# State-space layer of a four-layer trunk: input products of 64 states at a time, input copies divided by partitions, lagged copies placed behind the gelus, second half of the gate's product on other banks

## The chip, the cores and the metric

The kernel runs on one core of one Trainium2 chip. The metric is the device time of one execution in microseconds (us), here the median of three runs: 1214.68 us, from 1214.11 to 1215.03. One more execution was recorded by the hardware profiler; all rows quoted below come from that one.

Engines are named as the profile names them: PE is TensorE (PEld its weight loads), DVE is VectorE, ACT is ScalarE, POOL is GpSimd, SP is SyncE, which here only starts transfers.

## The reference

256 tokens of width 1024 pass through four layers. Each has a token mixer (stick-breaking attention, a chunked gating unit, a state-space layer, attention again) and a gated MLP. The change touches the third mixer alone:

```python
def s5_layer(xn, w_in, lam_re, lam_im, log_dt, b_re, b_im, c_re, c_im, d_skip, w_glu):
    u = (xn @ w_in).astype(jnp.float32)
    ug = u.reshape(B, L, SSM_GROUPS, SSM_GROUP)          # 64 groups of 16 channels, 64 states each
    ...
    bu_re = jnp.einsum('gph,blgh->blgp', bbar_re, ug)
    bu_im = jnp.einsum('gph,blgh->blgp', bbar_im, ug)
    ...
    _, _, xr, xi = lax.associative_scan(_complex_affine_combine, (a_re, a_im, bu_re, bu_im), axis=1)
    y = (jnp.einsum('ghp,blgp->blgh', c_re, xr) - jnp.einsum('ghp,blgp->blgh', c_im, xi))
    y = y.reshape(B, L, D_MODEL) + d_skip * u
    hg = jax.nn.gelu(y).astype(xn.dtype) @ w_glu
    a, g = jnp.split(hg, 2, axis=-1)
    return a * jax.nn.sigmoid(g)
```

## The kernel before

The whole trunk is one stream of instructions, written out by hand: every engine works through its own instructions in the order in which the Python code issues them, and an instruction waits only for the counters that its tiles need. So the order of calls in the code is the order on each engine. A tile from a pool with one buffer can be written again only when all readers of its last content are done.

**Large products.** A weight of 1 MB (128 x 2048 fp32) is loaded into one of three `raw` buffers by SP (line 40), rounded by ACT into `wh` (line 71, two halves), and DVE forms the remainder `wl` (line 72, two halves). `Weights.prep_to(i)` issues these for all weights up to the i-th; the load of a weight that needs a `raw` buffer starts when line 72 is through with the weight that held it. A product is three matmuls (`wh` with the high part, `wl` with the high part, `wh` with the low part: lines 132 to 134).

**The state-space layer** is class `S5`. Four tokens are taken together, so that the scan runs over 64 steps, and its body works in four parts of 16 groups, i = 0 to 3. Two of them share one buffer U[h].

- `ucopy(h)` copies the projected input from PSUM into U[h], 16 copies of 32 partitions x 256. For h = 0 ACT and DVE share them, for h = 1 ACT makes them all.
- `gmm(i)` multiplies the input by the input tables: for each of 8 columns a, real and imaginary part r, and block q of 32 states one matmul of 32 x 64.
- `scan(i)`, on DVE with a part on POOL, takes the two banks of `gmm(i)` and gives the state X[i], lines 1147 to 1171.
- `kmm(n)`, `kd(n)` and `kevac(n)` make the table of the lagged products inside a block of four tokens: matmuls (line 1180), a diagonal added by DVE (line 1185), and 16 copies by ACT (line 1192) into `kk[n]`; the tile of `kk[1]` is named `wl` in the rows.
- `ymm(i, parts)` forms the output of part i: its part `K_` uses `kk[i // 2]` and U, its part `X_` uses X[i] (all of it line 1205).
- `yevac(i)`: ACT applies the gelu (line 1213, tile `y`) and rounds it (line 1216, `gh`); DVE forms the remainder (line 1217, `gl`). The tile `y` comes from the pool of the layer, which has one buffer.
- `glu(c, n, acc, bs)` is the last product, 24 matmuls for both token blocks b, into the banks `acc[b]`. The four parts of the first output half use banks (0, 1) and (3, 4); `gate(b, ...)` then takes them out with a sigmoid on ACT (line 1284) and two steps on DVE (lines 1285 and 1286). The second half uses `self.acc`; its part 0 stands at the end of the body, its parts 1 to 3 in `tail`, first for b = 0, then for b = 1, and in between ACT and DVE do the norm of the next layer, whose transposes (line 179) go to two banks given in `run`.

In the body before, `kevac(0)` and `kevac(1)` stand inside `scan(0)` and `scan(1)`; `yevac(0)` and the splitting of the next weight stand ahead of `scan(2)`; the first half's two gates stand behind the splitting of all four weights of the second half; and b = 1 of the second half's part 0 writes banks 0 and 1, which the gate of b = 0 reads.

Of the kernel before, what the change touches and what calls it, by code (L numbers as in the profile page):

```python
# [21 lines left out]
class Weights:  # L22


    def __init__(self, nc, raw_p, hl_p, srcs, ahead_dma, ahead_prep):
        self.nc, self.raw_p, self.hl_p = nc, raw_p, hl_p
        self.srcs = srcs
        self.ad, self.ap = ahead_dma, ahead_prep
        self.raw, self.hl = {}, {}
        self.nd = self.npz = 0  # L30
        self.use = 0
# [66 lines left out]
class K:  # L98
# [131 lines left out]
    def run(self):  # L230
        nc, w = self.nc, self.w
        self.x = self.big.tile([128, 2, D], F32, name="x")
        self.ident = self.const.tile([128, 128], F32, name="ident")
        self.mhalf = self.const.tile([128, 1], F32, name="mhalf")
        nc.gpsimd.memset(self.mhalf[:, :], -0.5)
        zero = self.act_p.tile([128, 512], BF16, tag="gh", name="zero")
        nc.vector.memset(zero[:, :], 0.0)
        for c in (slice(0, 512), slice(512, D)):
            nc.sync.dma_start(self.x[:, 0, c], self.ins["x"][0][:, c])
        g = self.load_g(self.plan[0].g)  # L240
        nc.sync.dma_start(self.ident[:, :], self.ins["ident"])
        nc.sync.dma_start(self.x[:, 1], self.ins["x"][1])
        w.dma_to(3)

        def warm(n):

            for i in range(n):
                nc.tensor.matmul(self.bank(4), zero[:, 0:128], zero[:, :], start=True, stop=True)

        warm(12)  # L250
        self.s5 = next((p for p in self.plan if isinstance(p, S5)), None)
        prev = None
        nop = lambda: None
        for pi, ph in enumerate(self.plan + [None]):
            if prev:
                g = self.load_g(ph.g if ph else 8)
                prev.tail(0, nop)
                if ph:
                    w.prep_to(w.use + 2)
                xn0 = self.norm(0, g, prev.resid)  # L260
                if ph:
                    w.prep_to(w.use + 3)
                    prev.tail(1, lambda: (self.new_xt(), self.to_xt(0, xn0, (5, 6))))
                else:
                    nc.sync.dma_start(self.out[0], xn0[:, :])
                    prev.tail(1, nop)
                xn1 = self.norm(1, g, prev.resid)
                prev.close()
                if not ph:
                    for q, c in ((nc.sync, slice(0, 512)), (nc.scalar, slice(512, D))):  # L270
                        q.dma_start(self.out[1][:, c], xn1[:, c])
                    break
            else:
                xn = [self.norm(b, g) for b in range(2)]
                self.new_xt()
                w.half()
                self.xt_tr(0, xn[0], 0, 5)
                self.xt_evac(0, 0, 5)
                self.xt_tr(0, xn[0], 1, 6)
                warm(8)  # L280
                w.half()
                self.xt_tr(1, xn[1], 0, 0)
                self.xt_evac(1, 0, 0)
                self.xt_tr(1, xn[1], 1, 1)
                ph.open()
                h = ph.first()
                next(h)
                next(h)
                self.xt_evac(0, 1, 6)
                self.xt_evac(1, 1, 1)  # L290
                w.prep_to(2)
                ph.background()
                for _ in h:
                    w.step()
                Attn.consts(self)
                w.prep_to(w.use + 4)
                ph.body()
                prev = ph
                continue
            if ph is self.s5:  # L300
                self.s5.finish_tables()
            ph.open()
            if ph is self.s5:
                w.prep_to(w.use + 6)
            ph.head(0, lambda: self.to_xt(1, xn1, (0, 1)))
            w.prep_to(w.use + 2)
            ph.head(1, nop)
            w.prep_to(w.use + (3 if isinstance(ph, FFN) else 4))
            ph.body()
            prev = ph  # L310


class Phase:
    def __init__(self, k, i, g):
        self.k, self.i, self.g = k, i, g
        self.nc, self.ctx = k.nc, ExitStack()
# [415 lines left out]


class S5(Phase):
    def __init__(self, k, i, g):
        super().__init__(k, i, g)
        self.done = 0
        d = k.dram
        self.d_gt = d.tile([128, 2, 2, 2048], F32, name="d_gt")
        self.d_p = d.tile([128, 2, 2, 2048], F32, name="d_p")  # L740
        self.d_b = d.tile([128, 2048], F32, name="d_b")
        self.d_w = d.tile([8, 2, 32, 64], F32, name="d_w")
        self.d_t = [d.tile([128, 2048], F32, name=f"t{r}") for r in range(2)]
        self.d_s = d.tile([128, 1024], F32, name="d_s")
        self.par = k.const.tile([128, 19, 32], F32, name="spar")
# [355 lines left out]
    def body(self):  # L1101
        k, nc, w = self.k, self.nc, self.k.w
        ut = k.pst[:, 4:8, :].rearrange("p b (a t) -> p (b a) t", a=2)
        n = w.take()
# [17 lines left out]
        GT = [[v4(t[r]) for t in (gt0, gt1)] for r in range(2)]  # L1122
# [3 lines left out]
        X, U = {}, []  # L1126
        gb = lambda i, r: k.bank(((0, 1), (2, 5), (0, 1), (2, 7))[i][r])

        def gmm(i):

            for a in range(8):
                h, c = (8 * i + a) // 16, (8 * i + a) % 16
                for r in range(2):
                    for q in range(4):
                        nc.tensor.matmul(gb(i, r)[32 * q:32 * q + 32, 64 * a:64 * a + 64],
                                         GT[r][h][:, c, 32 * q:32 * q + 32], U[h][:, c, :],
                                         start=True, stop=True, skip_group_check=True)

        def scan(i, mid=lambda: None):
# [43 lines left out]
        def kd(n):  # L1183
            d = k.bank(3 + n).rearrange("p (a c) -> p a c", a=4)[:, :, 0:32]
            nc.vector.tensor_tensor(out=d, in0=d, in1=self.di[:, 4 * n:4 * n + 4], op=add)

        def kevac(n):
            kt = k.bank(3 + n).rearrange("p (a c) -> p a c", a=4)
            kk = self.kk[n][:, :, :, :].rearrange("p (a q) j c -> p q a (j c)", q=4)
            for jp in range(4):  # L1190
                for q in range(4):
                    nc.scalar.activation(kk[32 * jp:32 * jp + 32, q, :, 32 * jp:128],  # L1192
                                         kt[32 * q:32 * q + 32, :, 0:128 - 32 * jp], AF.Copy)
# [16 lines left out]
        def yevac(i):  # L1210
            p = k.bank(6 - i % 2)
            y = self.tmp.tile([128, 2, 256], F32, tag="y", name="y")
            nc.scalar.activation(y[:, :, :].rearrange("p m (c j) -> p m j c", j=4),
                                 p.rearrange("p (m j c) -> p m j c", m=2, j=4), AF.Gelu_apprx_tanh)
            g = self.gt[i] = k.new_gt()
            nc.scalar.activation(g[0][:, :, :], y[:, :, :], AF.Copy)
            nc.vector.tensor_tensor(out=g[1][:, :, :], in0=y[:, :, :], in1=g[0][:, :, :], op=sub)

        def ucopy(h, halves):
            d = U[h].rearrange("p (m r) c -> p m r c", m=4)  # L1220
            for pr in range(4):
                for j in range(4):
                    src = ut[32 * pr:32 * pr + 32, 4 * h:4 * h + 4].rearrange("p m (c j) -> p m c j", j=4)[:, :, :, j]
                    dst = d[32 * j:32 * j + 32, :, pr, :]
                    if halves and pr % 2:
                        nc.vector.tensor_copy(dst, src)
                    else:
                        nc.scalar.activation(dst, src, AF.Copy)
# [10 lines left out]
        scan(0, lambda: (kd(0), kevac(0)))  # L1239
        gmm(2)  # L1240
        kmm(1)
        scan(1, lambda: (kd(1), kevac(1)))
        ymm(0, K_ + X_)
        yevac(0)
        gmm(3)
        ymm(1, K_ + X_)
        w.prep_to(w.use + 2)
        scan(2)
        yevac(1)
        ymm(2, K_)  # L1250
        acc = [(k.bank(0), k.bank(1)), (k.bank(3), k.bank(4))]
        self.glu(0, w.take(), acc, (0, 1))
# [5 lines left out]
        self.glu(1, w.take(), acc, (0, 1))  # L1258
        ymm(3, X_)
        yevac(3)  # L1260
        for i in (2, 3):
            w.prep_to(w.use + 2)
            self.glu(i, w.take(), acc, (0, 1))
            w.step()
        for b in range(2):
            self.gate(b, acc[b], k.x[:, b, 0:512])
        self.acc = [(k.bank(2), k.bank(7)), (k.bank(0), k.bank(1))]
        self.glu(0, w.take(), self.acc, (0, 1))
        w.step()

# [105 lines left out]
```

## Time and profile before

| what | value |
|---|---|
| median of three runs | 1214.68 us |
| the profiled execution, its own time | 1214.6 us |
| its span, first to last instruction | 1212.8 us |
| PE busy | 1175.3 us, 97% of the span |
| DVE busy | 891.9 us, 74% |
| ACT busy | 705.7 us, 58% |
| POOL busy | 162.2 us, 13% |
| mean granted clock of PE | 0.994 of full speed |

A row of the timeline or of the chain of waits begins with the time from the start of the span and the duration, both in us. In a timeline row a bracket at the end gives the time for which the engine stood idle before it, and what ended that. "issue" is time in which PE waited for nothing that the profile shows.

### The profile page before, as it was taken

To read this page: it belongs to the slowest core of one execution; us is meant where nothing else is said; L and a number is where in the kernel's file an instruction comes from. 1 tells how busy PE (TensorE), PEld (TensorE's weight loads), DVE (VectorE), ACT (ScalarE), POOL (GpSimd) and SP (SyncE) were. 2 spreads that over 40 slices of the span, in tenths; PEclk is the share of its full clock that TensorE was granted. 3 is DMA by queue.
4 is the path that set the end of the run, shared out by engine and by line. 5 is a ranking of instruction groups with operands and counts; after the bars stand their busy time and mean duration, and the time that the engine had idled before them with its cause. 6 is when DMAs were issued, how large, how long until landed. Compare 5 with 4: busy or idle time off the path is not lost.

```text
span 1212.8 us, 22510 instructions
## 1 busy us (share of the span) xinstructions
PE 1175.3 (97%) x9328; PEld 1078.3 (89%) x9328; DVE 891.9 (74%) x1276; ACT 705.7 (58%) x1068; POOL 162.2 (13%) x308
## 2 busy tenths in 40 slices
PE   8999999999999999999967899999999999999997
PEld 5898999999898999999956699999988988999996
DVE  5665699789767599899478759876766656886673
ACT  5665576557554564668373657565555655665551
POOL 3885000000285001000111000000000000000000
PEclk8999999999999999999999999999999999999999
DMA  8623467787665356677761725645535332564530
GB/s 296 222 106 122 150 218 267 250 286 259 230 213 206 140 210 227 233 260 272 309 250 38 295 107 180 242 170 194 196 119 224 119 123 108 208 244 174 208 122 35
DMA packets 49559, 237.49 MB, mean 196 GB/s; under 512 B 14896, under 2 KB 15792, under 8 KB 24240
## 3 DMA queue, kind: packets, MB, share of 16 engines
q1 hardware_dynamic: 46208, 223.73, 51.4%
q0 software_dynamic: 3104, 12.06, 2.5%
q8 instruction: 73, 1.20, 0.4%
q14 instruction: 30, 0.25, 0.1%
q10 hardware_dynamic: 144, 0.26, 0.1%
HBM read 222.79 MB, written 13.24 MB: 195 GB/s over the span
## 4 chain that ended last, share of the span: by engine, by line
PE 91%; DVE 4%; ACT 2%; issue 1%; DMA 1%; POOL 0%; DVEq 0%; SPq 0%; POOLq 0%; ACTq 0%
PE pst L124 15%; PE pst L126 15%; PE pst L125 15%; PE pst L132 13%; PE pst L133 13%; PE pst L134 13%; PE pst L534 1%; PE pst L179 1%; DVE wl L72 1%; PE pst L510 1%; PE pst L551 1%; DVE wl L68 1%; ACT wl L1192 1%; DMA raw<-in_glu_dram 1%; DMA gb<-in_g_dram 1%
## 5 line engine op out<-in xcount | busy, mean ns | idle before, releaser
L72 DVE TENSOR_TENSOR wl<-raw,wh 128x1024 fp32r<-128x1024 f32 x344 | 414.8, 1231 | 58.7 <-ACT wh L71 58.5
L124 PE MATMUL pst<-xth,wh 128*128 128x256 f32 x1552 | 441.7, 285 | 0.0
L126 PE MATMUL pst<-xth,wl 128*128 128x256 f32 x1552 | 439.9, 283 | 0.0
L125 PE MATMUL pst<-xtl,wh 128*128 128x256 f32 x1552 | 439.9, 283 | 0.0
L71 ACT ACTIVATE wh<-raw 128x1024 fp32r<-128x1024 f32 x344 | 350.4, 1048 | 9.9 <-DMA raw<-in_glu_dram 4.4
L124 PEld LDWEIGHTS pst<-xth,wh 128*128 128x128 f32 x1552 | 298.1, 192 | 2.3
L125 PEld LDWEIGHTS pst<-xtl,wh 128*128 128x128 f32 x1552 | 298.2, 192 | 1.2
L126 PEld LDWEIGHTS pst<-xth,wl 128*128 128x128 f32 x1552 | 298.1, 192 | 0.0
L408 DVE SCALAR_TENSOR_TENSOR y<-pst,cw,y 128x255 f32<-128x255 f32 x352 | 160.8, 479 | 72.8 <-ACT y L404 66.5
L132 PE MATMUL pst<-wh,gh 128*128 128x512 f32 x512 | 202.5, 396 | 6.1 <-DVE gate L1285 4.5
L133 PE MATMUL pst<-wl,gh 128*128 128x512 f32 x512 | 200.8, 392 | 0.1
L134 PE MATMUL pst<-wh,gl 128*128 128x512 f32 x512 | 200.2, 391 | 0.0
L404 ACT ACTIVATE y<-pst,cw 128x256 f32<-128x256 f32 x176 | 88.0, 556 | 69.4 <-PE pst L126 64.8
L132 PEld LDWEIGHTS pst<-wh,gh 128*128 128x128 f32 x512 | 96.6, 189 | 26.3 <-DVE gate L1285 4.9
L134 PEld LDWEIGHTS pst<-wh,gl 128*128 128x128 f32 x512 | 96.6, 189 | 20.9 <-DVE gl L688 0.4
L133 PEld LDWEIGHTS pst<-wl,gh 128*128 128x128 f32 x512 | 96.8, 189 | 18.6 <-DVE wl L72 0.4
L132 PE MATMUL pst<-wh,xth 128*128 128x256 f32 (+1 forms) x336 | 106.1, 316 | 0.0
L134 PE MATMUL pst<-wh,xtl 128*128 128x256 f32 (+1 forms) x336 | 105.4, 314 | 0.0
L133 PE MATMUL pst<-wl,xth 128*128 128x256 f32 (+1 forms) x336 | 105.4, 314 | 0.0
L163 POOL TENSOR_TENSOR r<-m,mhalf 128x1 f32<-128x1 f32 x20 | 11.0, 552 | 687.6 <-DVE m L161 679.1
L414 ACT ACTIVATE y<-y 128x256 f32<-128x256 f32 x88 | 36.4, 419 | 76.2 <-DVE y L408 76.2
L198 ACT ACTIVATE gh<-y 128x256 fp32r<-128x256 f32 x88 | 36.1, 418 | 75.2 <-DVE y L415 75.2
(179 smaller groups left out, 1203.3 us busy)
## 6 DMA issues: line engine op xcount, KB each, us to landing
raw<-in_up_dram SPq DMA_DIRECT2D x88, 1024.0 KB, 4.9
raw<-in_down_dram SPq DMA_DIRECT2D x44, 1024.0 KB, 4.9
raw<-in_wqk_dram SPq DMA_DIRECT2D x16, 1024.0 KB, 5.4
raw<-in_wo_dram SPq DMA_DIRECT2D x8, 1024.0 KB, 4.8
raw<-in_glu_dram SPq DMA_DIRECT2D x8, 1024.0 KB, 7.0
raw<-in_wv_dram SPq DMA_DIRECT2D x7, 1024.0 KB, 6.1
gb<-in_g_dram SPq DMA_DIRECT2D x9, 512.0 KB, 5.7
d_gt<-gf POOLq DMA_DIRECT2D x4, 1024.0 KB, 8.1
```

What stands on the lines that cost most here:

```text
L71: nc.scalar.activation(h[:, s], r[:, s], AF.Copy)
L72: nc.vector.tensor_tensor(out=l[:, s], in0=r[:, s], in1=h[:, s], op=ALU.subtract)
L124: nc.tensor.matmul(out, h[:, cols], xh, start=first, stop=False, skip_group_check=True)
L125: nc.tensor.matmul(out, h[:, cols], xl, start=False, stop=False, skip_group_check=True)
L126: nc.tensor.matmul(out, l[:, cols], xh, start=False, stop=last, skip_group_check=True)
L132: nc.tensor.matmul(out, ah, h[:, cols], start=first, stop=False, skip_group_check=True)
L133: nc.tensor.matmul(out, ah, l[:, cols], start=False, stop=False, skip_group_check=True)
L134: nc.tensor.matmul(out, al, h[:, cols], start=False, stop=last, skip_group_check=True)
L198: self.nc.scalar.activation(g[0][:, j], src, AF.Copy)
L404: nc.scalar.activation(y[:, cs], p[:, cs], AF.Identity, scale=cw[:, s, m, 2:3], bias=cw[:, s, m, 3:4])
L408: nc.vector.scalar_tensor_tensor(y[:, o + tap:o + 256], p[:, o:o + 256 - tap], cw[:, s, m, 2 - tap:3 - tap], y[:, o + tap:o + 256], ALU.mu ...
L414: nc.scalar.activation(y[:, 256:512], y[:, 256:512], AF.Silu)
```

## The change

Six edits, all in the state-space layer and its hand-over:

1. `gmm` uses blocks of 64 states: two matmuls of 64 x 64 in place of four of 32 x 64.
2. `ucopy(0)` gives DVE the target partitions 64 to 127 (j = 2 and 3 of each pr) in place of every second pr.
3. `kevac(1)` leaves `scan(1)` and stands behind `yevac(0)`, `yevac(1)` and a `prep_to`.
4. `yevac(0)` moves from ahead of `gmm(3)` to behind `scan(2)`, and the `prep_to` from ahead of `scan(2)` to behind `yevac(1)`.
5. The last part of the first output half is computed for b = 0, its gate follows, then b = 1 and its gate; the splitting of the second half's later weights (`w.step()`) follows both gates.
6. The second half's b = 1 uses banks (5, 6) in place of (0, 1), and the next layer's first transposes go to (0, 1) in place of (5, 6).

```diff
-                    prev.tail(1, lambda: (self.new_xt(), self.to_xt(0, xn0, (5, 6))))
+                    prev.tail(1, lambda: (self.new_xt(), self.to_xt(0, xn0, prev.tb)))
...
 class Phase:
+    tb = (5, 6)
...
 class S5(Phase):
+    tb = (0, 1)
...
-                    for q in range(4):
-                        nc.tensor.matmul(gb(i, r)[32 * q:32 * q + 32, 64 * a:64 * a + 64],
-                                         GT[r][h][:, c, 32 * q:32 * q + 32], U[h][:, c, :],
+                    for q in range(2):
+                        nc.tensor.matmul(gb(i, r)[64 * q:64 * q + 64, 64 * a:64 * a + 64],
+                                         GT[r][h][:, c, 64 * q:64 * q + 64], U[h][:, c, :],
                                          start=True, stop=True, skip_group_check=True)
...
-                    if halves and pr % 2:
+                    if halves and j >= 2:
                         nc.vector.tensor_copy(dst, src)
...
-        scan(1, lambda: (kd(1), kevac(1)))
+        scan(1, lambda: kd(1))
         ymm(0, K_ + X_)
-        yevac(0)
         gmm(3)
         ymm(1, K_ + X_)
+        scan(2)
+        yevac(0)
+        yevac(1)
         w.prep_to(w.use + 2)
-        scan(2)
-        yevac(1)
+        kevac(1)
         ymm(2, K_)
         acc = [(k.bank(0), k.bank(1)), (k.bank(3), k.bank(4))]
         self.glu(0, w.take(), acc, (0, 1))
...
-        for i in (2, 3):
-            w.prep_to(w.use + 2)
-            self.glu(i, w.take(), acc, (0, 1))
-            w.step()
+        w.prep_to(w.use + 2)
+        self.glu(2, w.take(), acc, (0, 1))
+        w.prep_to(w.use + 2)
+        n = w.take()
         for b in range(2):
+            self.glu(3, n, acc, (b,))
             self.gate(b, acc[b], k.x[:, b, 0:512])
-        self.acc = [(k.bank(2), k.bank(7)), (k.bank(0), k.bank(1))]
+        w.step()
+        self.acc = [(k.bank(2), k.bank(7)), (k.bank(5), k.bank(6))]
```

Below, a row of the program's order gives line, operation, output and inputs; a bracket names the counters that the instruction waits for (Activation is ACT). The changed kernel's lines stand a few further on: 1192 is there 1196, 1213 is 1217, 1216 is 1220, 1217 is 1221, 1226 is 1230, 1228 is 1232, and the scan runs from 1151 to 1175.

ACT before, from the last copies into `kk[1]` to the second gelu:

```order
L1192 ACTIVATE wl_6468<-pst 32x4x64 x4
L1192 ACTIVATE wl_6468<-pst 32x4x32 x4
L1213 ACTIVATE y<-pst 128x2x4x64 [waits PE_49]
L1216 ACTIVATE gh<-y 128x512 [waits Activation_49]
L71 ACTIVATE wh_7186<-raw_6384 128x1024 [waits DMAHW7_49,DMAHW4_49]
L71 ACTIVATE wh_7186<-raw_6384 128x1024
L1213 ACTIVATE y<-pst 128x2x4x64 [waits DVE_49,PE_49]
```

ACT in the changed kernel, from the first gelu to the end of those copies:

```order
L1217 ACTIVATE y<-pst 128x2x4x64 [waits PE_49]
L1220 ACTIVATE gh<-y 128x512 [waits Activation_49]
L1217 ACTIVATE y<-pst 128x2x4x64 [waits DVE_49,PE_49]
L1220 ACTIVATE gh<-y 128x512 [waits Activation_49]
L71 ACTIVATE wh_7073<-raw_6384 128x1024 [waits DMAHW7_49,DMAHW4_49]
L71 ACTIVATE wh_7073<-raw_6384 128x1024
L1196 ACTIVATE wl_6468<-pst 32x4x128 [waits Pool_49]
L1196 ACTIVATE wl_6468<-pst 32x4x128 x3
L1196 ACTIVATE wl_6468<-pst 32x4x96 x4
L1196 ACTIVATE wl_6468<-pst 32x4x64 x4
L1196 ACTIVATE wl_6468<-pst 32x4x32 x4
```

The copies stood ahead of both gelus and now stand behind both, and behind the splitting of a weight. The second gelu waits for a DVE counter as well as for PE, before and now.

DVE before, from the last step of `scan(1)` to the first of `scan(2)`:

```order
L1171 TENSOR_TENSOR x_6915<-t_6885,x_6915 128x8x63 [waits DVE_49]
L1217 TENSOR_TENSOR gl<-y,gh 128x512 [waits Activation_49]
L72 TENSOR_TENSOR wl_7187<-raw_6384,wh_7186 128x1024 [waits DMAHW4_49,DMAHW0_49,Activation_49]
L72 TENSOR_TENSOR wl_7187<-raw_6384,wh_7186 128x1024 [waits Activation_49]
L1147 TENSOR_TENSOR t_7194<-pst,T_6537 128x512 [waits DMAHW7_49]
```

DVE in the changed kernel, from the last steps of `scan(2)` to the first of `scan(3)`:

```order
L1172 TENSOR_TENSOR x_7051<-t_7036,t_7038 128x8x63 [waits DVE_49,PE_49]
L1173 TENSOR_TENSOR x_7052<-t_7037,T_6538 128x8x63 [waits PE_49]
L1174 TENSOR_TENSOR t_7039<-t_7039,T_6537 128x8x63
L1175 TENSOR_TENSOR x_7052<-t_7039,x_7052 128x8x63 [waits DVE_49]
L1221 TENSOR_TENSOR gl<-y,gh 128x512 [waits Activation_49] x2
L72 TENSOR_TENSOR wl_7074<-raw_6384,wh_7073 128x1024 [waits DMAHW4_49,Activation_49]
L72 TENSOR_TENSOR wl_7074<-raw_6384,wh_7073 128x1024 [waits Activation_49]
L1151 TENSOR_TENSOR t_7153<-pst,T_6537 128x512 [waits PE_49]
```

`scan(2)` follows `scan(1)` at once now; the first remainder `gl`, which is the only DVE instruction that reads `y` there, stood ahead of `scan(2)` and now stands behind it.

ACT at the copies into U[0], in the changed kernel:

```order
L1232 ACTIVATE U<-pst 32x4x64 [waits PE_49,Activation_49]
L1232 ACTIVATE U<-pst 32x4x64
L1232 ACTIVATE U<-pst 32x4x64 [waits DVE_49]
L1232 ACTIVATE U<-pst 32x4x64
L1232 ACTIVATE U<-pst 32x4x64 [waits DVE_49]
L1232 ACTIVATE U<-pst 32x4x64
```

Before, ACT made four copies, waited for DVE's four, and made four more; now it makes two, waits for DVE's two, and so on, eight turns in place of four.

## Prediction

> **What bounds the kernel now.** I read the shares of the engines and of the chain of waits first, then the busy time of PE by stretches in the state-space layer, then the waits and the order of time there.
>
> ```profile
> PE 1175.3 (97%) x9328; PEld 1078.3 (89%) x9328; DVE 891.9 (74%) x1276; ACT 705.7 (58%) x1068; POOL 162.2 (13%) x308
> PE 91%; DVE 4%; ACT 2%; issue 1%; DMA 1%; POOL 0%; DVEq 0%; SPq 0%; POOLq 0%; ACTq 0%
> ```
>
> PE is the bound of the whole, so only time in which PE stands still or runs slowly can be won, and the 37.5 us that PE is not busy (1212.8 less 1175.3) are all that there is. The stretches of the layer, with PE alone:
>
> ```profile
> core 0: us, PE busy (x), PEclk, DMA share, GB/s
> 649.04:654.71 5.67, 5.67 (x28) 1.00 0.03 10
> 654.71:658.00 3.29, 3.10 (x193) 1.00 0.00 0
> 658.00:663.76 5.76, 5.76 (x28) 1.00 0.01 3
> 663.76:667.02 3.26, 2.13 (x128) 1.00 0.02 5
> 667.02:681.31 14.29, 14.18 (x67) 1.00 0.77 286
> 681.31:685.77 4.46, 0.00 (x1) 1.00 0.92 290
> 685.77:690.37 4.60, 4.60 (x13) 0.63 0.78 319
> 690.37:698.57 8.20, 8.20 (x38) 1.00 0.67 257
> 698.57:703.98 5.41, 5.41 (x26) 1.00 0.00 0
> ```
>
> These are, in turn: part 0 of the gate's product; `ymm(2, X_)` and `ymm(3, K_)`; part 1; `ymm(3, X_)`; parts 2 and 3 and the first token block of the second half's part 0 (60 matmuls); a standstill; the second block of that part (12 matmuls); the tail for b = 0 (36); two thirds of the tail for b = 1 (24). From 649.04 on PE has little to wait for. The reader is to see the standstill of 4.46 us and, behind it, 12 matmuls that take 4.60 us at a granted clock of 0.63. At 14.29 / 60 = 0.238 us each they would take 2.86, so the slow clock costs 1.74.
>
> ```profile
> 674.55 6.51 DMA raw<-in_glu_dram
> 684.39 0.61 ACT gate L1284
> 685.02 0.70 DVE gate L1285
> 685.77 0.50 PE pst L132
> ...
> PE pst L1205 <- issue: 5.9, 4, 2.1
> PE pst L132 <- DVE gate L1285: 4.5, 1, 4.5
> PE pst L1205 <- DVE x L1171: 0.8, 1, 0.8
> ```
>
> The chain shows why: PE waits for the gate to empty banks 0 and 1, the gate stands on ACT behind weights, and these wait for a load. Ahead of 649.04 the order on ACT and DVE decides when PE may start part 0:
>
> ```profile
> 632.76 7.02 ACT L1192 ACTIVATE wl<-pst 32x512 f32<-32x512 f32 x16 [2.40 <-DVE pst L1185]
> 639.81 1.14 ACT L1213 ACTIVATE y<-pst 128x512 f32<-128x512 f32 x1
> 640.99 0.63 ACT L1216 ACTIVATE gh<-y 128x512 fp32r<-128x512 f32 x1
> 641.52 1.99 ACT L71 ACTIVATE wh<-raw 128x1024 fp32r<-128x1024 f32 x2
> 648.25 1.13 ACT L1213 ACTIVATE y<-pst 128x512 f32<-128x512 f32 x1 [4.74 <-PE pst L1205]
> ...
> 629.11 0.68 DVE L1147 TENSOR_TENSOR t<-pst,T 128x512 f32<-128x512 f32 x1
> 632.37 0.30 DVE L1185 TENSOR_TENSOR pst<-pst,di 128x128 f32<-128x128 f32 x1 [0.78 <-PE pst L1180]
> 638.96 0.68 DVE L1171 TENSOR_TENSOR x<-t,x 128x504 f32<-128x504 f32 x1
> 641.65 0.69 DVE L1217 TENSOR_TENSOR gl<-y,gh 128x512 fp32r<-128x512 f32 x1 [2.00 <-ACT gh L1216]
> 644.87 0.68 DVE L1147 TENSOR_TENSOR t<-pst,T 128x512 f32<-128x512 f32 x1
> 654.41 0.68 DVE L1171 TENSOR_TENSOR x<-t,x 128x504 f32<-128x504 f32 x1
> ```
>
> The 16 copies into `kk[1]` (7.02 us) are done at 639.78, nine microseconds ahead of their reader `ymm(2, K_)`, which stands on PE right ahead of part 0. `scan(1)` ends at 639.64, and `scan(2)` starts only at 644.87, behind `gl` and a weight; it takes 654.41 + 0.68 - 644.87 = 10.22.
>
> **The change, part by part.**
>
> *The copies into U[0]* stay one after the other. The order shows that ACT waits for DVE and DVE for ACT after every two copies, as they did after every four.
>
> ```profile
> L1228 ACT ACTIVATE U<-pst 32x256 f32<-32x256 f32 x24 | 9.0, 374 | 5.7 <-PE pst L366 3.6 <-DVE U L1226 1.8
> L1226 DVE COPY U<-pst 32x256 f32<-32x256 f32 x8 | 3.4, 423 | 17.3 <-ACT U L1228 17.2
> 611.18 0.38 ACT U L1228
> 611.59 0.42 DVE U L1226
> ```
>
> Sixteen copies take 8 x 0.374 + 8 x 0.423 = 6.4 us either way, and a turn costs 611.59 - 611.56 = 0.03, four times more: 0.1. ACT's last copies now end two DVE copies (0.85) ahead of the end in place of four (1.7), so the weight that ACT splits next comes up to 0.85 later, and DVE needs it ahead of `scan(0)`. Between 0 and 1.0 later in all; I take 0.3, since half of DVE's part of that weight can start on the first half.
>
> *The input products* fall from 256 to 128 in the program. No row has 64 x 64; the nearest are these, on either side:
>
> ```profile
> 616.71 1.32 PE pst L1135 x80
> 618.03 1.75 PE pst L1180 x64
> ```
>
> Rows of 32 x 64 follow each other in 1.32 / 80 = 0.0165 us, rows of 32 x 128 in 1.75 / 64 = 0.027. Four `gmm` have 512 such rows; at half the rows and one to two times 0.0165 each, PE gains between 0 and 4.2 us, and some of the "issue" standstill (5.9 us, four times about 2) may go too. None of it moves the end: until 649.04 PE runs ahead of ACT and DVE. What it does is to have `kmm(1)` ready before DVE asks, so the 0.78 goes; at worst it stays. `scan(1)` thus ends at 639.64 + 0.3 - 0.78 = 639.2 (638.9 to 640.6).
>
> *The lagged copies.* On DVE `scan(2)` follows at 639.2 and ends at 649.4. `gl` of part 0 stands behind it and ends at 649.4 + 0.69 = 650.1. The tile `y` has one buffer, so the second gelu may not write it before that `gl` has read it: this is the DVE counter in its row of the order. Before, it found `gl` done (642.3) and waited for PE; now it waits for the scan. Queued behind it on ACT are its rounding, a weight and the 16 copies into `kk[1]`; behind these, on PE, `ymm(2, K_)` and all parts of the gate's product. From a gelu to the end of the weight behind it ACT took 641.52 + 1.99 - 639.81 = 3.70, so the copies start at 653.8 and end at 660.8. PE follows them copy by copy; I add 0.5, half of the 64 rows of `ymm(2, K_)`. Part 0 starts at 661.3 in place of 649.04: **+12.3**.
>
> *From there on* PE has the same work in one piece. X[2] (649.4) and X[3] are ready early: DVE does `gl`, a weight and `scan(3)` by about 666, PE needs X[3] at 661.3 + 5.67 + 3.29 + 5.76 = 676. So the waits of 663.76 to 667.02 go: 3.26 - 2.13 = **-1.13**.
>
> *Gate and banks.* Nothing in part 0 of the second half reads or writes a bank of the first half's gates any more: **-4.46**, and the slow clock behind it: **-1.74**. A gate of b = 0 behind part 3 of b = 0 adds no wait on PE.
>
> *The clock at the restart.* Between about 642 and 661 PE has only the few rows that follow the copies. In this trace a standstill of 4.46 us was followed by 1.74 us of loss; one twice as long and more should bring at least the same. The bounds are 0 and twice that, 3.5; I take one such loss, the only one that a row shows: **+1.74**. [...]
>
> *What is late next* is the hand-over. The weights for the tail are now split behind the gates, and the loads of the next layer's first weights start when DVE is through with those.
>
> ```profile
> raw<-in_up_dram SPq DMA_DIRECT2D x88, 1024.0 KB, 4.9
> 698.57 0.60 ACT L1284 ACTIVATE gate<-pst 128x512 f32<-128x512 f32 x1 [8.70 <-PE pst L134]
> 702.28 1.42 DVE L155 SCALAR_TENSOR_TENSOR xn<-x,r,gb 128x512 f32<-128x512 f32 x2 [0.66 <-POOL r L163]
> 703.98 0.87 PE pst L179 x8
> ```
>
> Before, ACT and DVE were free for the gate at 698.57, the norm was ready at 703.70 and PE came to its transposes at 703.98: a margin of 0.28. Now two weights of the next layer stand ahead of that gate. With a landing of 4.9 us they are split about when PE ends the tail of b = 0, with 6.51 (the chain's load) some 1.6 later. So between 0 and 1.7 us of new wait, and I take **+0.4**. That the transposes use banks 0 and 1 costs nothing: both were emptied 20 us earlier.
>
> The sum is 12.3 - 1.13 - 4.46 - 1.74 + 1.74 + 0.4 = +7.1, on the profiled execution's 1214.6 (span 1212.8): **1221.7 us**. The median of the runs is 0.08 higher, which I leave out.
>
> **The rivals.**
>
> 1. *The second gelu does not wait for the scan*, because the counter that it waits for is an earlier one. Then it follows `ymm(1)`: X[1] at 639.2, two products of 64 rows (2.1) and perhaps one "issue" standstill, about 642.4; the copies end at 642.4 + 3.70 + 7.02 = 653.1, part 0 starts at 653.6, +4.6. The sum is 4.6 - 1.13 - 4.46 - 1.74 + 1.74 + 0.4 = -0.6: 1214.0, not slower. It decides at a start of part 0 at 654.2, where gains and losses meet. The order speaks against it: there is a DVE counter in that row, and `gl` alone reads `y` on DVE.
> 2. *The copies into U[0] run side by side*, as divided partitions suggest: 3.4 us in place of 6.4, and everything up to the second gelu is 3.0 earlier: 1218.7. The waits of the order speak against it.
> 3. *The hand-over costs more*: loads that start later and DVE's splitting fall behind PE by one load, 3 to 5 us in place of 0.4: 1224 to 1226. For it speaks the load of 6.51; against it, that the tail has 8.20 us of work ahead of the gate.
>
> **How the numbers follow.** My forecast has 0.76: `y`'s wait is in the program. Its own range is 1219 to 1225: scans 0.3 earlier to 1.4 later, clock 0 to 3.5, hand-over 0 to 1.7, not all at one end. Rival 1 has 0.09, rival 2 0.07, rival 3 0.08. The range of 1217.5 to 1225.5 leaves out rival 1, half of rival 3 and a little of the rest. A measurement of this kernel can tell about 0.2% (2.4 us) from no change. Slower by more than that, above 1217.1: the forecast, rivals 2 and 3 nearly whole, 0.88; within: most of rival 1 and the lower edge of rival 2, 0.08; faster: 0.04.
>
> **What would show it.** In the profile after: `scan(2)` starting within 0.5 us of the end of `scan(1)`; the second gelu starting behind `gl`, about 10 us after the end of `scan(1)`; the 16 copies ending near 661 and part 0 starting half a microsecond later; a granted clock near 0.6 in the stretch behind that; no wait of PE for line 1292, the gate; eight turns at the copies into U[0]. I am wrong if the second gelu follows PE, if the clock stays at 1.00, or if PE waits again at the transposes of the norm.

## Result, and the profile after

| | median | range | runs | ratio to before, 95% |
|---|---|---|---|---|
| before | 1214.39 us | 1213.84 to 1215.03 | 4 | |
| changed | 1221.68 us | 1219.52 to 1222.41 | 4 | 1.0055 [1.0042, 1.0068] |
| changed, measured again later | 1220.05 us | 1219.83 to 1221.93 | 4 | 1.0049 [1.0032, 1.0066] |

The change makes the kernel slower by about half a per cent. The profiled execution of the changed kernel took 1219.52 us (span 1217.7). The shares of the engines and of the chain, after:

```profile
PE 1184.1 (97%) x9072; PEld 1082.9 (89%) x9072; DVE 891.2 (73%) x1276; ACT 705.6 (58%) x1068; POOL 162.9 (13%) x308
PE 92%; DVE 4%; DMA 1%; ACT 1%; POOL 1%; issue 1%; SPq 0%; DVEq 0%; POOLq 0%; ACTq 0%
```

They hardly tell the two kernels apart: PE is busy for 97% of the span in both, though one takes 5 us more. The waits of the state-space layer tell them apart (engine, line, what it waited for; us in total, times, longest):

```profile
ACT y L1217 <- DVE gl L1221: 13.3, 1, 13.3
PE pst L1209 <- ACT wl L1196: 12.2, 4, 11.6
PE pst L1209 <- issue: 3.6, 3, 1.7
DVE t L1163 <- POOL x L1169: 2.7, 4, 0.7
```

PE's wait of 4.5 us for the gate is gone. In its place ACT waits 13.3 us for `gl`, once, and PE waits 11.6 us for ACT's copies. The order of time shows that these two are one wait:

```profile
634.24 1.15 ACT L1217 ACTIVATE y<-pst 128x512 f32<-128x512 f32 x1 [4.06 <-PE pst L1209]
...
632.28 2.34 DVE L1163 TENSOR_TENSOR_SCAN t<-mg,t 128x512 f32<-128x512 f32 x2 [0.67 <-POOL x L1169]
637.87 0.68 DVE L1175 TENSOR_TENSOR x<-t,x 128x504 f32<-128x504 f32 x1
638.47 0.68 DVE L1151 TENSOR_TENSOR t<-pst,T 128x512 f32<-128x512 f32 x1
648.01 0.68 DVE L1175 TENSOR_TENSOR x<-t,x 128x504 f32<-128x504 f32 x1
648.61 0.68 DVE L1221 TENSOR_TENSOR gl<-y,gh 128x512 fp32r<-128x512 f32 x1
649.39 1.07 ACT L1217 ACTIVATE y<-pst 128x512 f32<-128x512 f32 x1 [13.34 <-DVE gl L1221]
652.91 7.19 ACT L1196 ACTIVATE wl<-pst 32x512 f32<-32x512 f32 x16
653.54 0.42 PE L1209 MATMUL pst<-U,wl 128*32 128x64 f32 x2 [11.63 <-ACT wl L1196]
661.36 0.80 PE L132 MATMUL pst<-wh,gh 128*128 128x512 f32 x1
```

`scan(2)` follows `scan(1)` at once (638.47). The first `gl` stands behind it (648.61), the second gelu behind that `gl` (649.39), the copies into `kk[1]` behind the gelu (652.91 to 660.10), and part 0 behind the copies (661.36). The stretches from there to the next layer's transposes, PE alone:

```profile
core 0: us, PE busy (x), PEclk, DMA share, GB/s
661.36:667.91 6.55, 6.55 (x25) 0.86 0.01 3
667.91:670.73 2.82, 2.82 (x193) 1.00 0.02 6
670.73:676.39 5.66, 5.66 (x30) 1.00 0.08 12
676.39:678.32 1.93, 1.93 (x130) 1.00 0.85 323
678.32:708.46 30.14, 30.14 (x139) 1.00 0.67 256
```

These are part 0, the products of `ymm(2, X_)` and `ymm(3, K_)`, part 1, `ymm(3, X_)`, and the 132 matmuls of parts 2 and 3, the second half's part 0, the tail for b = 0 and two thirds of b = 1. (A stretch counts every row that touches it: part 0 has 24 matmuls and stands there with 25.) Here the change does what it was laid out for: from part 0 to the transposes PE takes 47.10 us, against 54.78 before (703.82 - 649.04). It starts that piece so much later that this doesn't pay.

### The profile page after: what moved, and what is told of

Same layout as the page of the kernel before. It is cut to its first block, busy times and chain, and to the rows that moved or that the text cites. A ratio compares the mean times of both kernels' runs of the same rounds, so it can differ in the third digit from the quotient of the medians.

```text
span 1217.7 us, 21996 instructions
## 1 busy us (share of the span) xinstructions
PE 1184.1 (97%) x9072; PEld 1082.9 (89%) x9072; DVE 891.2 (73%) x1276; ACT 705.6 (58%) x1068; POOL 162.9 (13%) x308
## 3 DMA queue, kind: packets, MB, share of 16 engines
q8 instruction: 71, 1.16, 0.4%
## 4 chain that ended last, share of the span: by engine, by line
PE 92%; DVE 4%; DMA 1%; ACT 1%; POOL 1%; issue 1%; SPq 0%; DVEq 0%; POOLq 0%; ACTq 0%
PE pst L124 15%; PE pst L126 15%; PE pst L125 15%; PE pst L132 14%; PE pst L134 13%; PE pst L133 13%; PE pst L536 1%; PE pst L179 1%; PE pst L512 1%; DMA wh<-d_p 1%; PE pst L553 1%; PE pst L1209 1%; DVE wl L68 1%; DVE wl L72 1%; DVE t L1163 1%
## 5 line engine op out<-in xcount | busy, mean ns | idle before, releaser
L72 DVE TENSOR_TENSOR wl<-raw,wh 128x1024 fp32r<-128x1024 f32 x344 | 414.7, 1230 | 57.6 <-ACT wh L71 57.6
```

Of the source, the lines that this page charges most:

```text
L72: nc.vector.tensor_tensor(out=l[:, s], in0=r[:, s], in1=h[:, s], op=ALU.subtract)
```

## The experiments

Each kernel is an edit of the kernel before or of the changed one. Executions differ by up to 1.8 us ahead of this layer's body, which no edit touches (its first copy starts at 608.87 us in one and at 610.70 in another), so the times of the traces are compared from the first copy into U[0], worked out here from the start times in each profile. "To part 0" runs from that copy to part 0's first matmul, "rest" from there to the transposes (line 179); the times are in us.

| kernel | time of the profiled execution | to part 0 | part 0 | rest, with part 0 | sum | against before |
|---|---|---|---|---|---|---|
| before | 1214.6 | 39.01 | 5.67 | 54.78 | 93.79 | |
| changed | 1219.52 | 52.49 | 6.55 | 47.10 | 99.59 | +5.80 |
| e9, changed | 1219.95 | 52.28 | 7.03 | 47.68 | 99.96 | +6.17 |
| e10, changed | 1221.54 | 52.50 | 7.42 | 48.06 | 100.56 | +6.77 |
| e1 | 1213.29 | 44.50 | 6.24 | 47.32 | 91.82 | -1.97 |
| e2 | 1207.40 | 37.20 | 5.66 | 49.91 | 87.11 | -6.68 |
| e3 | 1209.06 | 33.07 | 14.54 | 55.99 | 89.06 | -4.73 |
| e4 | 1222.83 | 54.94 | 5.66 | 46.52 | 101.46 | +7.67 |
| e4b | 1223.62 | 52.45 | 5.67 | 49.40 | 101.85 | +8.06 |
| e5 | 1213.98 | 36.55 | 5.84 | 56.86 | 93.41 | -0.38 |
| e7 | 1209.26 | 35.08 | 5.65 | 52.59 | 87.67 | -6.12 |
| e8 | 1205.54 | 35.34 | 6.52 | 48.73 | 84.07 | -9.72 |

Each row is one execution. The kernel before has one profile only, and e2, whose instructions up to part 0 are those of the kernel before, reaches part 0 1.81 us earlier. So a difference of that size against before, in the column "to part 0", can be a difference between two executions.

**e1: another tile for the second gelu.** The changed kernel, where the odd gelus write into a tile that no `gl` ahead of them reads:

```diff
-            y = self.tmp.tile([128, 2, 256], F32, tag="y", name="y")
+            y = self.tmp.tile([128, 2, 256], F32, tag="y", name="y") if i % 2 == 0 else \
+                self.t0[:, 0:512].rearrange("p (m t) -> p m t", m=2)
```

> The changed kernel with one thing more: the gelus of parts 1 and 3 write into the table tile of scan(0), which is free by then, so that the second gelu need not wait for gl of part 0. Theory (the one-buffer tile y ties the second gelu to the end of scan(2)): in the time base of the profile after, the second gelu follows ymm(1) at about 642 in place of 649.4, the copies into kk[1] end at about 652.8, part 0 of the gate's product starts at about 653.4 in place of 661.4, and the time falls by 8.0 to about 1213.7 us. Rival (the copies are late because they stand behind two gelus and a weight, whatever buffer y has, or gl behind the scan holds part 0 by itself): part 0 starts no earlier than 660 and the time stays above 1220.

Measured: 1214.11 us (10 runs), ratio 0.9998 [0.9989, 1.0008]. ACT's order of time in its profile:

```profile
642.91 1.08 ACT L1218 ACTIVATE t<-pst 128x512 f32<-128x512 f32 x1 [5.09 <-PE pst L1209]
644.56 1.99 ACT L71 ACTIVATE wh<-raw 128x1024 fp32r<-128x1024 f32 x2
646.45 7.21 ACT L1196 ACTIVATE wl<-pst 32x512 f32<-32x512 f32 x16
```

The gelu now waits for PE and no longer for DVE, and everything behind it comes 8.0 us earlier (44.50 against 52.49), as expected. So the wait for the tile `y` is 8.0 of the 13.5 us by which part 0 was late, and without it the kernel is as fast as before. Part 0 still starts 5.5 us later than before, since the copies stand behind the second gelu and a weight; the gain behind part 0 makes up for that. The time is also that of the prediction's first rival, put at 1214.0.

**e2: the gates and banks alone.** The kernel before with edits 5 and 6 of the change: the lines of its diff with `tb`, and all those behind `yevac(3)`, of which these are the last:

```diff
-        self.acc = [(k.bank(2), k.bank(7)), (k.bank(0), k.bank(1))]
+        w.step()
+        self.acc = [(k.bank(2), k.bank(7)), (k.bank(5), k.bank(6))]
```

> The kernel before with edits 5 and 6 alone: first half's gates per token block, ahead of the second half's weights, and the second half's b = 1 on banks 5 and 6. Theory: PE's wait of 4.46 us and the slow clock behind it (1.74) go, the hand-over to the norm costs about 0.4: 1214.4 - 5.8 = 1208.6 us. Rival (another wait takes its place: weights of the tail split too late, or the norm of the next layer): a new standstill of 2 us or more behind part 3, and 1211 us or more.

Measured: 1208.60 us (4 runs), ratio 0.9955 [0.9940, 0.9970]. Among the waits of PE that are left behind part 0 are these two:

```profile
PE pst L1209 <- DVE x L1175: 1.2, 2, 0.8
PE pst L179 <- DVE xn L155: 0.3, 1, 0.3
```

The gate's 4.5 us and the slow clock behind them are gone (the granted clock is 1.00 in every stretch of 2 us from 630 to 710), and a new wait of 0.3 stands at the hand-over: 5.9 us under before's 1214.54, where the three terms -4.46, -1.74 and +0.4 make -5.8. In the profile 4.87 us of the gain lie behind part 0 (49.91 against 54.78), where the two edits act; the other 1.81 lie ahead of it, where the instructions are the same. Some of this is one effect: PE, being earlier, waits longer for X[2] and X[3] (1.7 us in place of 1.1). The change contains the gain; its other half costs more.

**e3: the copies back in `scan(1)`.** The changed kernel, its edit 3 undone:

```diff
-        scan(1, lambda: kd(1))
+        scan(1, lambda: (kd(1), kevac(1)))
...
-        kevac(1)
```

> The changed kernel with edit 3 alone undone: kevac(1) again inside scan(1), ahead of both gelus. Theory (the place of the copies behind the second gelu is the whole loss): the copies end near 638, part 0 then waits only for gl of part 0 behind scan(2) and starts near 649.3 in place of 661.4, PE waits up to 0.6 for X[3]; about 1210 us. Rival (gl behind scan(2) by itself costs as much, so that the place of the copies matters little): part 0 starts after 655 and the time is above 1216.

Measured: 1210.22 us (6 runs), ratio 0.9965 [0.9953, 0.9976]. From ACT's and PE's order of time:

```profile
649.24 1.08 ACT L1217 ACTIVATE y<-pst 128x512 f32<-128x512 f32 x1 [9.31 <-DVE gl L1221]
...
641.98 0.50 PE L132 MATMUL pst<-wh,gh 128*128 128x512 f32 x1
649.20 0.80 PE L134 MATMUL pst<-wh,gl 128*128 128x512 f32 x1 [6.49 <-DVE gl L1221]
```

The second gelu still waits for `gl`, but nothing that part 0 needs is queued behind it, so the wait costs far less. What is left is that PE itself needs that `gl`, behind `scan(2)`: 6.49 us inside part 0, and about 2.4 us more there, since the granted clock is 0.69 in the 7.32 us behind this wait. So part 0 did not start near 649.3, as expected, but began earlier and waited inside; the time came out as expected. The loss of the change has two causes in series, the late `gl` and the copies queued behind the gelu that waits for it; taking away either one takes back 7.6 us (e1) or 11.5 us (e3) of the first median, 1.6 us less of the second.

**e4 and e4b: PE kept busy ahead of part 0.** The changed kernel with matmuls that nobody reads, 92 ahead of `ymm(2, K_)` and some between its rows:

```diff
+                            if fill and m == 0:
+                                busy((4, 3, 2, 1)[j])
...
-        ymm(2, K_)
+        busy(92)
+        ymm(2, K_, 1)
```

In e4b the four numbers are 2, 1, 0, 0.

> The changed kernel with about 130 extra bf16 matmuls of 128 x 256 into a free bank between ymm(1) and part 0 of the gate's product, which add nothing to the output: PE does not idle there, nothing else is moved. Theory (the long standstill lets the clock fall and the restart is paid at half clock, by an amount that differs from run to run): granted clock 1.00 behind part 0's start, part 0 in 5.7 in place of 6.6 us, median 1 to 2 us lower (about 1220.2) and a spread below 1.5 us. Rival (the clock costs nothing here, the spread has another cause): 1221.7 and a spread as before, near 3 us.

> The changed kernel with extra matmuls that nobody reads, as in e4_pe_kept_busy, but with only 2, 1, 0 and 0 of them behind the K_ matmuls of the four column blocks, so that PE does not fall behind the copies into kk[1]. Theory (the idle stretch ahead of part 0 costs a restart at half clock): part 0 starts about 0.5 us behind the last copy, as in the changed kernel, its 28 matmul rows take 5.7 us in place of 6.6, and the time is about 1 us under the changed kernel's, 1220.7. Rival (the restart costs nothing that counts, since the later stretch has slack): same time as the changed kernel, 1221.7.

Measured: e4 1222.62 us (4 runs), ratio 1.0069 [1.0052, 1.0086]; e4b 1221.93 us (4 runs), 1.0056 [1.0040, 1.0071]. The clock and the length of part 0 came out as expected in both, and e4's four runs lie within 0.8 us; the times were missed, and e4b's four runs are 3.5 us apart. PE's stretch of part 0 and two of its rows in e4b:

```profile
663.15:668.82 5.67, 5.67 (x27) 1.00 0.00 0
...
672.72 0.64 PE L1214 MATMUL pst<-U,wl 128*32 128x64 f32 x29 [1.37 <-issue]
712.55 1.32 PE L179 MATMUL pst<-ident,xn 128*128 128x128 f32 x8 [1.43 <-DVE xn L155]
```

In part 0 the clock is 1.00, and it takes 5.66 and 5.67 us, as before the change. So the slow clock at part 0, 0.75 to 0.86 in three profiles of the changed kernel, depends on what PE does ahead of it. The two kernels differ there: in e4 the clock is 1.00 in every stretch of 2 us from 628 to part 0, while in e4b it falls behind a wait of 2.10 us for the copies and comes back only at part 0, though PE shows hardly any idle time between:

```profile
656.00:658.00 2.00, 2.00 (x11) 0.55 0.45 70
660.00:662.00 2.00, 2.00 (x21) 0.50 0.21 86
662.00:664.00 2.00, 2.00 (x40) 0.74 0.00 0
```

So e4b moved the slow clock out of part 0 but did not take it away, and what makes the clock fall there is not shown. No time was won in either: in e4 the fill itself held PE up (part 0 at 54.94 in place of 52.49); in e4b the 0.9 won in part 0 stands against a standstill of 1.37 that waits for nothing the profile shows, and one of 1.43 at the hand-over. That last one follows a load that lands late: ACT begins the norm right behind this row, in the changed kernel and then in e4b:

```profile
701.20 2.01 ACT L71 ACTIVATE wh<-raw 128x1024 fp32r<-128x1024 f32 x2 [0.51 <-DMA raw<-in_up_dram]
```

```profile
705.30 2.01 ACT L71 ACTIVATE wh<-raw 128x1024 fp32r<-128x1024 f32 x2 [1.82 <-DMA raw<-in_up_dram]
```

What the restart costs in the whole time is thus not settled by e4 and e4b, only what it costs in part 0.

**e9 and e10: the changed kernel twice more**, to see where its runs differ.

> The changed kernel, not edited, for a second profile: its first profiled execution took 1219.52 us, while the median is 1221.68. Theory (the restart): an execution near 1222 shows part 0's 28 matmul rows at 7.5 to 8.7 us in place of 6.6, at half clock for longer. Rival (hand-over): part 0 as before at 6.6 us, and PE's wait for the norm's result at 2 to 3 us in place of 0.6, behind a load that lands later. Second rival (ahead of part 0): both as in the first profile, and the second gelu 1 to 2 us later against the first copy into U[0].

> The changed kernel once more, not edited, for a third profile, with the same expectations as e9_changed_again: one of part 0's stretch, the wait for the norm's result and the start of the second gelu moves with the time.

Measured: the 1220.05 us of the first table for e9 (its profiled execution 1219.95), and 1221.54 for e10. Part 0, in e9 and then in e10:

```profile
661.23:668.26 7.03, 7.03 (x25) 0.80 0.01 2
```

```profile
662.43:669.85 7.42, 7.42 (x25) 0.75 0.01 2
```

With the first profile's 6.55 at 0.86, the restart cost 0.9, 1.4 and 1.8 us over the 5.67 of full clock: the same program, three prices. Behind part 0 the three agree (40.55, 40.65 and 40.64 us). The other difference lies ahead of the body: its first copy stands at 608.87, 608.95 and 609.93. So of the 2.0 us between the fastest and the slowest of the three, 0.9 is the clock (a part of what the theory expected, and less than its 7.5 to 8.7 us of part 0), and 1.06 lies ahead of the body, which none of the three expectations named; the hand-over did not move.

**e5: the input products alone.** The kernel before with edit 1:

```diff
-                    for q in range(4):
+                    for q in range(2):
```

> The kernel before with edit 1 alone (input products of 64 states). Theory: PE has fewer rows, but until part 0 it runs ahead of ACT and DVE, and the wait of scan(1) for kmm(1) (0.78 us) is replaced by one for POOL's subtraction (0.67 us in the changed kernel's profile); so the time is within 0.2% of before, about 1214.2. Rival (the wait of 0.78 goes without another in its place, and PE's saved 2 to 4 us count in part): 1211 to 1213.5.

Measured: 1214.21 us (11 runs), ratio 0.9996 [0.9987, 1.0005]. Of PE's waits, before and then in e5:

```profile
PE pst L1135 <- issue: 7.1, 3, 3.1
PE pst L1205 <- issue: 5.9, 4, 2.1
PE pst L1180 <- issue: 1.5, 1, 1.5
```

```profile
PE pst L132 <- DVE gate L1285: 4.5, 1, 4.5
PE pst L1205 <- issue: 3.6, 3, 1.6
PE pst L132 <- DVE t L1154: 3.6, 1, 3.6
PE pst L1205 <- DVE x L1171: 2.0, 3, 0.8
```

PE lost 14.5 us to "issue" in this layer before, and 3.6 with the larger blocks: a saving of 10.9 us of standstill that the time does not show. (e2, with the small blocks, lost 4.5 + 5.9 + 0.9 = 11.3, so the saving differs between executions.) PE comes to part 0 6.1 us earlier, but to a bank that `scan(2)` still reads: it waits 3.6 and starts only 2.5 earlier. Behind that it waits longer for the scans (2.0 in all in place of 1.1), and the gate's wait is still there. With the larger blocks the order of ACT and DVE ends this stretch, not PE.

**e7: the first gelu and the copies ahead of `scan(2)`.** The changed kernel with

```diff
         ymm(0, K_ + X_)
+        yevac(0)
+        kevac(1)
         gmm(3)
         ymm(1, K_ + X_)
         scan(2)
-        yevac(0)
         yevac(1)
         w.prep_to(w.use + 2)
-        kevac(1)
```

> The changed kernel with the first gelu and its remainder ahead of gmm(3) and scan(2) again, and the copies into kk[1] behind that first gelu, ahead of the second. Theory (the loss of the change is the remainder standing behind scan(2), not that the copies are late): the second gelu waits for PE or for ACT's own copies alone, part 0 starts near 646 to 648 us, the wait for the gate's banks stays away, and one wait for X[3] of about 1 to 2 us comes back; time about 1207.5, against 1208.6 of the gate edits alone. Rival (the copies are late wherever they stand behind a gelu): part 0 near 654, time about 1213.

**e8: the same, with POOL's subtraction later.** In each scan POOL's copy and memset of the tile `mg`, which the subtraction doesn't need, go ahead of it:

```diff
+            mg = self.tmp.tile([128, 8, 64], F32, tag="mg", name="mg")
+            nc.gpsimd.tensor_copy(mg[:, :, :], self.par[:, 0, ps].unsqueeze(2).to_broadcast([128, 8, 64]))
+            nc.gpsimd.memset(mg[:, :, 0:1], 0.0)
             V(out=A(0), in0=b[0], in1=T[0], op=mul)
             V(out=A(1), in0=b[1], in1=T[1], op=mul)
             G(out=A(0), in0=A(0), in1=A(1), op=sub)
-            mg = self.tmp.tile([128, 8, 64], F32, tag="mg", name="mg")
-            nc.gpsimd.tensor_copy(mg[:, :, :], self.par[:, 0, ps].unsqueeze(2).to_broadcast([128, 8, 64]))
-            nc.gpsimd.memset(mg[:, :, 0:1], 0.0)
```

> As e7_copies_between_gelus, with the other products of a scan ahead of A(0), A(1) and POOL's subtraction, so that the copy and memset of the shifted state stand ahead of that subtraction on POOL. Theory: the 0.67 us for which DVE waits for POOL in each scan goes, X[3] comes about 2 us earlier, and PE's wait for X[3] goes: 1205 to 1206. Rival (PE has no wait left that depends on the scans): same as e7_copies_between_gelus.

The expectation speaks of products that go ahead; the edit leaves DVE's order as it is and moves those two steps of POOL alone.

Measured: e7 1207.18 us (4 runs), ratio 0.9941 [0.9927, 0.9954]; e8 1206.16 us (4 runs), 0.9932 [0.9919, 0.9946]. Both beat both kernels, by 7.3 and 8.3 us against the 1214.45 of before measured beside them. The waits for X[3] in e7 and in e8:

```profile
662.21 1.10 PE L1209 MATMUL pst<-x,wh 128*32 128x64 f32 x64 [2.16 <-DVE x L1172]
664.12 1.94 PE L1209 MATMUL pst<-x,wl 128*32 128x64 f32 x64 [0.80 <-DVE x L1175]
```

```profile
661.03 1.10 PE L1209 MATMUL pst<-x,wh 128*32 128x64 f32 x64 [0.21 <-DVE x L1172]
662.93 1.10 PE L1209 MATMUL pst<-x,wl 128*32 128x64 f32 x64 [0.80 <-DVE x L1175]
```

In e7 the second gelu waits for nothing (644.91, right behind ACT's copies) and part 0 starts at 35.08, earlier than before's 39.01; X[3] is late next. In e8 DVE's four waits for POOL (2.7 us in e7) are gone, and PE's first wait for X[3] is down from 2.16 to 0.21. The 1.0 us between their medians lies within the intervals, so that e8 is faster than e7 is seen in these waits only, not in the time. The profiles differ by more than the waits, for e7's execution, the slowest of its four, also lost clock behind them (e8 lost 0.9 us to it in part 0, at 6.52, with a granted clock of 0.59 from 646 to 648):

```profile
664.00:666.00 2.00, 1.88 (x65) 0.50 0.00 0
668.00:670.00 2.00, 2.00 (x7) 0.50 0.85 336
```

## Why the prediction was right, point by point

The predicted 1221.7 us stands beside 1221.68 and 1220.05. The mechanism was the one put down: e1 took the wait away and came out at 1214.11, and e2 measured the gain of the gates and banks. The terms, in us against before, from the first copy into U[0]:

| term | predicted | changed | e9 | e10 |
|---|---|---|---|---|
| start of part 0 | +12.3 | +13.48 | +13.27 | +13.49 |
| restart at half clock | +1.74 | +0.88 | +1.36 | +1.75 |
| all else up to the transposes | -6.93 | -8.56 | -8.46 | -8.47 |
| sum | +7.1 | +5.80 | +6.17 | +6.77 |

The predicted "all else" is -1.13 - 4.46 - 1.74 + 0.4. Some errors were hidden in the sum:

- *The copies into U[0]* took their turns as predicted. `scan(0)` ended 0.4 later from the first copy, where 0.3 was taken.
- *What ends the stretch ahead of part 0.* The prediction has PE run ahead of ACT and DVE until 649.04. In the profile before, PE waits for nothing but "issue" from 617 on, seven times, the last 1.5 us ahead of part 0 (1.67 us, ended at 647.58), and it reaches part 0 without a wait. So before the change it was PE, with its standstills, that set 649.04, and the input products do move that time (e5). It did no harm here, since in the changed kernel the copies end this stretch by far. The 37.5 us that PE is not busy are not all that there is either: the 1.74 us of slow clock lie in its busy time.
- *`scan(1)`* should have ended 0.78 earlier, since `kmm(1)` is ready in time. That wait went, but DVE waits 0.67 for POOL at line 1163 (the row at 632.28), which the earlier wait had covered: before, the same step of `scan(1)` started at 633.36 without a wait. With the 0.3 of the copies, the end of `scan(1)` was put at -0.48 and measured at +0.07: 638.55 against 639.64, with a body that began 1.16 earlier. The step named no wait that comes next on DVE; it should have. In e2's profile the 0.78 is gone too, with the small blocks, so it was not a fixed part of the kernel before.
- *From the copies to part 0* half a microsecond was added, and 1.26 measured (660.10 to 661.36). PE's rows of `ymm(2, K_)` run at a granted clock of 0.50 there; the step took PE to be following copy by copy at full speed. In e7, where the clock is 1.00 at this place, the same distance is 0.74 (644.88 to 645.62).
- *The restart* cost 0.9 to 1.75. The term of 1.74, taken from the one case in the trace before, turned out to be the upper end of what the three profiles show, and the granted clock in part 0 was 0.75 to 0.86 in place of the expected 0.6. Why one program has several prices is not shown. Most of the slow stretch lies ahead of part 0: PE's first row behind the wait is at 653.54, and its rows run at a granted clock of 0.50 from there to about 663.2 in the first profile (0.99 from there to the end of part 0). That is 9.7 us, of which the last 1.8 lie in part 0, with PE paced by the copies in the first 6.6.
- *Behind part 0* the gain was 1.5 to 1.6 larger than predicted. 0.2 is `ymm(3, X_)` (3.26 to 1.93, where 1.13 was taken), 0.47 the products ahead of part 1 (3.29 to 2.82, of which 0.19 was "issue"), 0.1 part 1. The rest, 0.86, lies in the 132 matmuls: 36.80 to 30.14, -6.66 in place of -5.8. The hand-over was counted there at +0.4; at 30.14 / 132 = 0.228 a matmul, no such wait is to be seen in these three profiles, while e4 has 0.25, e2 0.34, e1 0.46, e3 0.83 and e4b 1.43. What the other 0.46 are is not shown.

So a start of part 0 put 1.0 to 1.2 too early met a gain behind it put 1.5 to 1.6 too small, and a restart that cost up to 0.9 less. The agreement to a few hundredths is luck, the more so as the +13.3 to +13.5 are counted from one execution of the kernel before, and from e2's 37.20 they would be 1.8 larger; that the sign and the size came out is not luck. No run tried the copies into U[0] by themselves.

Of the rivals, the first (the gelu does not wait) did not happen, and its time was confirmed by e1. The second (the copies into U[0] side by side) fell: their turns are in the trace. The third (a dearer hand-over) did not show in the changed kernel, though e4b's rows fit its mechanism, a load that lands late.

## What to carry to other kernels

Before work is moved behind another engine's long step, look for what else on that engine reads a tile with one buffer: here one `gl` of 0.68 us, moved behind a scan of 10 us, held the next writer of its tile, and with it 16 copies that had nothing to do with either. Price a wait by what is queued behind the waiting instruction, not by its own length. And when a change has several edits, time them apart: this one contained 5.9 us of gain and covered it with a start about 13 us later.

## What the hardware showed that was not expected

Half as many rows of twice the width saved PE no time of their own. One `gmm`, from its first row (lines 1139 and 1135) to the first of the next product, in the changed kernel (64 rows of 64 x 64) and then before (128 rows of 32 x 64, with a standstill):

```profile
633.56 0.64 PE L1209 MATMUL pst<-x,wl 128*32 128x64 f32 x28 [1.23 <-issue]
634.13 0.34 PE L1139 MATMUL pst<-U,wh 128*64 128x64 f32 x4
...
636.15 0.75 PE L1209 MATMUL pst<-U,kk 128*32 128x64 f32 x36
637.57 0.58 PE L1209 MATMUL pst<-U,kk 128*32 128x64 f32 x26 [0.67 <-issue]
```

```profile
637.07 0.23 PE L1135 MATMUL pst<-U,wh 128*32 128x64 f32 x3
639.91 0.24 PE L1135 MATMUL pst<-U,wh 128*32 128x64 f32 x1 [2.11 <-issue]
641.17 0.23 PE L1205 MATMUL pst<-U,kk 128*32 128x64 f32 x3
```

They take 2.02 us, and 641.17 - 637.07 - 2.11 = 1.99 us. What the larger blocks save is the standstills marked "issue": 14.5 us in the layer before (11.3 in e2), 4.3 after (3.6 and 0.7). They come in stretches of many small matmuls and at even distances: from the one that ends at 633.56 to the next at 637.57 PE does 28 + 64 + 36 = 128 matmuls, each with a weight load of its own (the profile has 9072 of either). Between the seven of the kernel before lie 125 to 131 matmuls each time, between the four of the changed kernel 252, 128 and 127. What PE waits for in them (0.7 to 3.1 us each) is not shown, and no run tried that by itself.
